# A hybrid decoder trunk on one core: three paddings that put the tensor engine's operands at one address modulo 512 bytes

## The chip, the cores and the metric

The kernel runs on one core of a Trainium2 chip. The metric is device time in microseconds (us) of one execution; the time before is 1634.1 us, the median of three runs between 1632.56 and 1635.3 us. TensorE (PE) multiplies, VectorE (DVE) and ScalarE (ACT) do the elementwise work, GpSimd (POOL) a little, and SyncE (SP) issues the loads and stores. The profile shows PE's weight loads as a row of their own (PEld).

## The reference

One decoder layer over 1024 rows of width 1024, then a final norm. All is float32.

```python
h = rms_norm(x, norm_mix)
proj = h @ w_in                      # 8 groups of 1024 columns: xa ga q f v g m_a m_b
xa = causal_depthwise_conv(xa, conv_w, conv_b)          # 4 taps
y_a = rg_lru(xa, w_r, b_r, w_i, b_i, lam) * gelu(ga)    # gates: 4 blocks of 256x256, then a scan
o = rms_norm(hgrn2_chunkwise(silu(q), k(f), log_f(f), v), hg_norm)
y = sigmoid(m_a) * y_a + sigmoid(m_b) * (o * silu(g))
x = x + y @ w_out
h = rms_norm(x, norm_mlp)
x = x + square(relu(h @ w_up)) @ w_down                 # width 4096 between
return rms_norm(x, norm_final)
```

## The kernel before, in words

**Three products for one.** Each float32 operand of the large products is split in two rounded parts: ScalarE writes the high part (L76), VectorE the rest (L77). `mm3` (L115, L116, L117) then issues three matmuls for one product: high with low, high with high, low with high. In `PE.matmul(o, a, b)` the operand `a` is the stationary one, which a weight load brings into the array (128 columns, 512 bytes of each partition), and `b` is the moving one, which is streamed through (512 columns, 2048 bytes of each partition, in nearly all of these matmuls; 256 columns for `pv`). A matmul's weight load runs while the matmul before it streams.

**The mixer** (tiles `pj_*`, `pv`, `pr`, `pi`, `sc`, `po`). Two chunks of 512 rows, in each four passes over 256 columns of every group. A projection (`pj_xa`, `pj_q`, `pj_f`, `pj_g`, `pj_mb`, `pj_ga`, `pj_ma`) has a slice of `w_in` (`wH`, `wL`) stationary and the transposed normed rows (`hT0H`, `hT0L`) moving. The convolution leaves its result in `xc`, split in `xcH` and `xcL`; these are the moving operand of the two gate products `pr` and `pi` of the recurrence (192 matmuls in all). The chunkwise mixer works with float32 matmuls that are not split (`sc`, `pk`, `pkv`, `po`). The output projection (`po`) has the mixer's result `y` stationary and the weights moving.

**The MLP** is done by Strassen's scheme in Winograd's form: seven products for eight, over 16 quads of the hidden width. In the first part (tiles `uX`, `uY`, `uZ`) the moving operands are the seven combinations of the normed rows (`h2B11`, `h2t1`, `h2T3` and so on, a high and a low tile each), which lie in four pools at the top of SBUF for the whole part; the stationary ones are the split weights (`wA..`, `ws..`) at its bottom. That is 16 quads x 7 steps x 4 x 3 = 1344 matmuls. In the second part (tiles `dX`, `dY`, `dZ`; 1344 matmuls again) two quads are accumulated together: three matmuls of the one quad, whose operands both lie in the lower pools, alternate with three of the other, whose operands both lie in pools at the top (`late_u`, `late_w`, `late_w1`). Here a `u` tile is stationary and a weight tile moving; VectorE adds each finished bank to the output rows `acc` (L963).

**Order and place.** The tile framework orders the instructions by the program's text and by priorities, and lays tiles in a pool one after the other; pools opened with `side="right"` are stacked downward from the top of SBUF. The tile `pad` (L674) is never read: it is opened first on that side and only shifts what is opened after it. The pool `mix` holds the mixer's tiles in the order of their first use: `mf` and `mu` come first, the two `xp` buffers of the convolution (L300) lie just before `xcH` and `xcL`.

Of the kernel before, what the change touches and what calls it, by code (L numbers as in the profile page):

```python
# [10 lines left out]
F32 = mybir.dt.float32  # L11
# [7 lines left out]
P = 128  # L19
D = 1024  # L20
S = 1024
T = 512
# [19 lines left out]
def trunk(ctx: ExitStack, tc: tile.TileContext, x, wts, mlp, pv, gains, mask_f, mask_u, out):  # L42
# [8 lines left out]
    def opened(name, **how):  # L51
        cm = tc.tile_pool(name=name, bufs=1, reuse_waits="tile", **how)
        return cm.__enter__(), lambda: cm.__exit__(None, None, None)
# [21 lines left out]
    def split(src, h, lo):  # L75
        keep(A.copy(h, src))  # L76
        keep(V.tensor_tensor(out=lo, in0=src, in1=h.bitcast(F32), op=ALU.subtract))  # L77
# [92 lines left out]
    def mt(tag, name, shape=(P, T), dt=F32, bufs=1):  # L170
        return m.tile(list(shape), dt, tag=tag, name=name, bufs=bufs)

    mf = mt("mf", "mf", (P, 32))
    mu = mt("mu", "mu", (P, 7, 8, 32), U8)

    def small_inputs():
# [93 lines left out]
    def project(c, name):  # L270

        pp = [bank("pj", f"pj_{name}_{s}") for s in range(2)]
        for half in range(2):
            wh, wl = next_w()
            for k in range(4):
                hh, hl = kt(hT[c], 4 * half + k)
                for s in range(2):
                    cols = slice(k * 256 + s * P, k * 256 + (s + 1) * P)
                    mm3(pp[s], wh[:, cols], wl[:, cols], hh, hl, half == 0 and k == 0, half == 1 and k == 3)
        return pp  # L280
# [15 lines left out]
    def conv(c, p, pp):  # L296
        xc = mt("xc", f"xc{c}{p}", (P, 2, T))
        for s in range(2):
            u = 2 * p + s
            xp = mt("xp", f"xp{c}{u}", (P, T + 3), bufs=2)  # L300
            V.tensor_copy(xp[:, 0:3], xcar[:, u, :])
            A.copy(xp[:, 3 : T + 3], pp[s])
            A.activation(
                xc[:, s, :],
                pp[s],
                AF.Identity,
                bias=pvt[:, PV_CB + u : PV_CB + u + 1],
                scale=pvt[:, PV_CW + 24 + u : PV_CW + 25 + u],
            )
            for j in range(3):  # L310
                V.scalar_tensor_tensor(  # L311
                    xc[:, s, :],
                    xp[:, j : j + T],
                    pvt[:, PV_CW + 8 * j + u : PV_CW + 8 * j + u + 1],
                    xc[:, s, :],
                    op0=ALU.mult,
                    op1=ALU.add,
                )
            if c + 1 < NC:
                G.tensor_copy(xcar[:, u, :], xp[:, T : T + 3])  # L320
        xh = mt("xcH", f"xcH{c}{p}", (P, 2, T), F32R)
        xl = mt("xcL", f"xcL{c}{p}", (P, 2, T), F32R)
        split(xc, xh, xl)
        return xc, xh, xl
# [43 lines left out]
    def f_of(c, p, pp):  # L368
        ff = mt("f", f"f{c}{p}", (P, 2 * T))
        kk = mt("kk", f"kk{c}{p}", (P, 2 * T))  # L370
        for s in range(2):
            u = 2 * p + s
            f, k = ff[:, s * T : (s + 1) * T], kk[:, s * T : (s + 1) * T]
            A.activation(f, pp[s], AF.Sigmoid)
            A.activation(k, pp[s], AF.Sigmoid, scale=-1.0)
            V.tensor_scalar(f, f, omlb[:, u : u + 1], lb[:, u : u + 1], op0=ALU.mult, op1=ALU.add)
            V.tensor_scalar(k, k, omlb[:, u : u + 1], None, op0=ALU.mult)
        V.tensor_scalar(ff, ff, F_MIN, 1.0, op0=ALU.max, op1=ALU.min)
        return ff, kk
# [246 lines left out]
    for c in range(NC):  # L626
        if c == 0:
            first_norm(0)
            mu32 = small_inputs()
        else:  # L630
            out_proj(0, ys, res0, done0, lambda: first_norm(1))
        ys = a2_set(a2y, f"y{c}")
        for p in range(NPAIR):
            v = project_v(c, f"{c}{p}")
            px = project(c, f"xa{c}{p}")
            if c == 0 and p == 0:
                parameters()
                tc.keep_in_program_order(V.tensor_copy(mu, mu32.to_broadcast([P, 7, 8, 32])))
            xc3 = conv(c, p, px)
            q1 = q_of(c, p, project(c, f"q{c}{p}"))  # L640
            f, kk = f_of(c, p, project(c, f"f{c}{p}"))
            with tc.high_priority(300):
                h = rg_lru(c, p, *xc3)
            on = hgrn(c, p, q1, f, kk, v)
            gates(c, p, h, on, ys)
# [25 lines left out]


    pad, close_pad = opened("pad", side="right")
    pad.tile([P, 8], F32, tag="pad", name="pad")  # L674

    h2p = [opened(f"h2{i}", side="right") for i in range(4)]
    HOME = {"T4": 0, "B22": 0, "T3": 0, "B21": 1, "n2": 2, "t1": 2, "B11": 3}
# [371 lines left out]
```

## Time and profile before

| | |
|---|---|
| median of 3 runs | 1634.1 us |
| span of the profiled execution, first to last instruction | 1630.3 us |
| time of a run beyond that span (median less span) | 3.8 us |
| PE busy | 1585.8 us, 9240 matmuls |
| PE weight loads busy | 1303.6 us, 9240 |
| VectorE busy | 1211.9 us |
| ScalarE busy | 762.2 us |
| GpSimd busy | 62.8 us |

The profiled execution's time is its span with some us around it, and these 3.8 us stand for them here. The span divides into the mixer with the two output projections (from 0 to about 985 us), the first part of the MLP (to about 1305) and the second (to the end). Matmuls are pipelined: the duration of one in a row (some 0.39 us) is longer than the time from its start to the next one's start (some 0.23 us), and it is the second that adds up to the span. Where two matmuls of the same shape follow their own kind without a wait, a longer start-to-start time shows as the same number of ns more in the duration.

### The profile page before, as it was taken

To read this page: it belongs to the slowest core of one execution; us is meant where nothing else is said; L and a number is where in the kernel's file an instruction comes from. 1 tells how busy PE (TensorE), PEld (TensorE's weight loads), DVE (VectorE), ACT (ScalarE), POOL (GpSimd) and SP (SyncE) were. 2 spreads that over 40 slices of the span, in tenths; PEclk is the share of its full clock that TensorE was granted. 3 is DMA by queue.
4 is the path that set the end of the run, shared out by engine and by line. 5 is a ranking of instruction groups with operands and counts; after the bars stand their busy time and mean duration, and the time that the engine had idled before them with its cause. 6 is when DMAs were issued, how large, how long until landed. Compare 5 with 4: busy or idle time off the path is not lost.

```text
span 1630.3 us, 23190 instructions
## 1 busy us (share of the span) xinstructions
PE 1585.8 (97%) x9240; PEld 1303.6 (80%) x9240; DVE 1211.9 (74%) x1751; ACT 762.2 (47%) x1186; POOL 62.8 (4%) x99
## 2 busy tenths in 40 slices
PE   7999999999999999999999998999999999999998
PEld 6788788788788788788787876888888878888886
DVE  5975956848764965848759688977777888888876
ACT  4643545435442544436435566767766732221113
POOL 0010100100100000000100000000000000000000
PEclk9999999999999999999999998999999999999999
DMA  6222223223244222222222352666666566666652
GB/s 236 91 66 91 91 66 103 66 91 93 78 165 142 80 77 91 78 84 98 66 91 91 125 200 102 262 247 239 233 248 247 216 259 237 238 246 249 252 207 104
DMA packets 57996, 246.51 MB, mean 151 GB/s; under 512 B 6688, under 2 KB 6816, under 8 KB 47136
## 3 DMA queue, kind: packets, MB, share of 16 engines
q1 hardware_dynamic: 56304, 239.27, 40.8%
q10 hardware_dynamic: 1584, 5.77, 1.0%
q8 instruction: 72, 1.18, 0.3%
q14 instruction: 36, 0.29, 0.1%
HBM read 185.24 MB, written 59.77 MB: 150 GB/s over the span
## 4 chain that ended last, share of the span: by engine, by line
PE 82%; DVE 15%; issue 1%; ACT 1%; DMA 1%; POOL 0%; DVEq 0%; POOLq 0%; SPq 0%; ACTq 0%
PE dX L115 4%; PE dX L117 4%; PE dX L116 4%; PE uX L115 3%; PE uX L117 3%; PE uX L116 3%; DVE wL L77 2%; PE pj_ga L117 2%; PE pj_ga L116 2%; PE pj_ga L115 2%; PE pj_ma L117 2%; PE pv L116 2%; PE pv L115 2%; PE pj_ma L116 2%; PE pv L117 2%; PE pj_f L117 2%
## 5 line engine op out<-in xcount | busy, mean ns | idle before, releaser
L77 DVE TENSOR_TENSOR wL<-raw,wH 128x1024 fp32r<-128x1024 f32 x160 | 194.4, 1215 | 151.3 <-ACT wH L76 148.7
L76 ACT CAST wH<-raw 128x1024 fp32r<-128x1024 f32 x160 | 167.9, 1050 | 166.9 <-issue 67.1
L963 DVE TENSOR_TENSOR acc<-acc,dX 128x512 f32<-128x512 f32 x128 | 86.7, 682 | 29.6 <-PE dX L117 28.9
L76 ACT CAST wA<-q 128x512 fp32r<-128x512 f32 x32 | 19.8, 621 | 130.9 <-PE dX L117 82.8
L963 DVE TENSOR_TENSOR acc<-acc,dY 128x512 f32<-128x512 f32 x64 | 43.6, 683 | 16.6 <-PE dY L117 14.9
L345 DVE RECIPROCAL rr<-rr 128x512 f32<-128x512 f32 x16 | 53.5, 3345 | 0.0
L823 ACT ACTIVATE b<-b 128x512 f32<-128x512 f32 x48 | 30.2, 631 | 38.7 <-DVE b L822 38.6
L115 PE MATMUL pv<-wL,hT0H 128*128 128x256 f32 x128 | 37.1, 289 | 0.0
L117 PE MATMUL pv<-wH,hT0L 128*128 128x256 f32 x128 | 36.7, 286 | 0.0
L116 PE MATMUL pv<-wH,hT0H 128*128 128x256 f32 x128 | 36.6, 286 | 0.0
L115 PE MATMUL pv<-wL,hT1H 128*128 128x256 f32 x128 | 36.5, 285 | 0.0
L116 PE MATMUL pv<-wH,hT1H 128*128 128x256 f32 x128 | 36.2, 283 | 0.0
L117 PE MATMUL pv<-wH,hT1L 128*128 128x256 f32 x128 | 36.2, 283 | 0.0
L311 DVE SCALAR_TENSOR_TENSOR xc<-xp,pvt,xc 128x512 f32<-128x512 f32 x48 | 33.1, 746 | 0.0
L551 ACT ACTIVATE on<-po 128x128 f32<-128x128 f32 x64 | 17.0, 278 | 33.5 <-PE po L541 33.2
L570 ACT ACTIVATE smb<-pj_mb 128x512 f32<-128x512 f32 x16 | 9.6, 597 | 45.4 <-PE pj_mb L117 45.2
L824 ACT ACTIVATE b<-b 128x512 f32<-128x512 f32 x48 | 30.0, 629 | 1.1
L384 DVE TENSOR_TENSOR seg<-seg 128x128 f32<-128x128 f32 (+2 forms) x96 | 26.8, 309 | 0.2
L565 ACT ACTIVATE g<-pj_g 128x512 f32<-128x512 f32 x16 | 9.6, 598 | 37.2 <-PE pj_g L117 37.2
L444 POOL TENSOR_SCALAR seg<-seg 128x128 f32<-128x128 f32 (+1 forms) x16 | 12.6, 790 | 360.9 <-DVE seg L384 360.9
L117 PE MATMUL pj_ga<-hT1H,wL 128*128 128x512 f32 x64 | 26.5, 414 | 0.0
L115 PE MATMUL uX<-h2B11L,wA 128*128 128x512 f32 x64 | 26.2, 409 | 0.3 <-DVE rstd_h L137 0.3
(1854 smaller groups left out, 5258.3 us busy)
## 6 DMA issues: line engine op xcount, KB each, us to landing
raw<-wts_in SPq DMA_DIRECT2D x160, 512.0 KB, 3.5
q<-mlp_in SPq DMA_DIRECT2D x64, 512.0 KB, 4.0
x<-x_in SPq DMA_DIRECT2D x8, 512.0 KB, 5.6
acc<-x ACTq DMA_DIRECT2D x8, 512.0 KB, 6.0
y_out<-acc SPq DMA_DIRECT2D x16, 256.0 KB, 2.1
xs<-x_in SPq DMA_DIRECT2D x8, 256.0 KB, 4.2
x<-xs SPq DMA_DIRECT2D x8, 256.0 KB, 2.1
x2s<-x_in SPq DMA_DIRECT2D x4, 512.0 KB, 4.8
```

Of the source, the lines that this page charges most:

```text
L76: keep(A.copy(h, src))
L77: keep(V.tensor_tensor(out=lo, in0=src, in1=h.bitcast(F32), op=ALU.subtract))
L115: PE.matmul(o, ah, bl, start=first, stop=False, **how)
L116: PE.matmul(o, ah, bh, start=False, stop=False, **how)
L117: PE.matmul(o, al, bh, start=False, stop=last, **how)
L311: V.scalar_tensor_tensor(xc[:, s, :], xp[:, j : j + T], pvt[:, PV_CW + 8 * j + u : PV_CW + 8 * j + u + 1], xc[:, s, :], op0=ALU.mult, op1= ...
L345: V.reciprocal(rec, rec)
L384: mul = lambda o, a, b: V.tensor_tensor(out=o, in0=a, in1=b, op=ALU.mult)
L551: A.activation(on[:, 4 * s + n, :], po[:, n * P : (n + 1) * P], AF.Square, accum_out=ssq[:, 4 * s + n : 4 * s + n + 1])
L823: A.activation(b[:, at, :], b[:, at, :], AF.Relu, scale=-1.0 if at == 2 else 1.0)
L824: A.activation(b[:, at, :], b[:, at, :], AF.Square)
L963: V.tensor_tensor(out=dst, in0=dst, in1=banks[bk, pr], op=op)
```

## The change

Three tiles grow. `mf` goes from 32 to 64 columns, of which the first 32 are used; each of the two `xp` buffers goes from T + 3 = 515 to T + 64 = 576 columns, of which the first 515 are used; `pad` goes from 8 to 56 columns, none of which is used.

```diff
-    mf = mt("mf", "mf", (P, 32))
+    mf = mt("mf", "mf", (P, 64))[:, 0:32]
...
-            xp = mt("xp", f"xp{c}{u}", (P, T + 3), bufs=2)
+            xp = mt("xp", f"xp{c}{u}", (P, T + 64), bufs=2)
...
     pad, close_pad = opened("pad", side="right")
-    pad.tile([P, 8], F32, tag="pad", name="pad")
+    pad.tile([P, 56], F32, tag="pad", name="pad")
```

Every engine issues the same instructions in the same order as before, with the same shapes and waits; only addresses differ. In the built programs the start addresses, modulo 512 bytes, are:

| tiles | before | after |
|---|---|---|
| `hT`, `y`, `wH`, `wL`, the lower pools' weights and `u` tiles, `raw`, `s`, `b`, `e` | 256 | 256 |
| `h2..` (moving operands of the MLP's first part) | 448 | 256 |
| the upper pools' weights and `u` tiles (one quad of two in the second part), `acc` | 448 | 256 |
| `xcH`, `xcL` (moving operands of `pr` and `pi`) | 192 | 256 |
| `q1`, `kk`, `qa`, `seg`, `dd`, `h`, `rw`, `ri`, `rr` | 192 | 256 |
| `x`, `xn`, `f`, `xc`, `v`, `kT`, `g1`, `g2`, `on`, `scT`, `tmp` | 128 | 256 |
| `sn` (moving in some `po`) | 256 | 320 |
| `ident` (moving in transposes) | 128 | 128 |

Counted from the bottom of a partition, `hT`, `y` and the operands of the lower pools lie below byte 113408, `xcH` and `xcL` from 170688, and `h2` and the operands of the upper pools from 114624 up.

All offsets of the split operands inside their tiles are multiples of 512 bytes, so each matmul of `mm3` starts its two operands where the table says: before, `pj` and `pv` at 256 and 256, `pr` and `pi` at 192 (moving) and 256, `u` at 448 (moving) and 256, `d` at 256 and 256 for the one quad and 448 and 448 for the other; after, all at 256 and 256.

## The prediction

> **What bounds the kernel now.** I read the page's totals first, then its chain of work that ended last.
>
> ```profile
> span 1630.3 us, 23190 instructions
> PE 1585.8 (97%) x9240; PEld 1303.6 (80%) x9240; DVE 1211.9 (74%) x1751; ACT 762.2 (47%) x1186; POOL 62.8 (4%) x99
> PEclk9999999999999999999999998999999999999999
> PE 82%; DVE 15%; issue 1%; ACT 1%; DMA 1%; POOL 0%; DVEq 0%; POOLq 0%; SPq 0%; ACTq 0%
> ```
>
> TensorE is the bound: 97% busy, at full clock, and 82% of the chain. The change removes no instruction and no wait, so it can only act through what a matmul takes. The next view is the groups of matmuls by line and shape: count, busy us, mean ns of one.
>
> ```profile
> L115 PE MATMUL pj_q<-hT0L,wH 128*128 128x512 f32 x64 | 24.9, 389 | 0.0
> L115 PE MATMUL pi<-xcL,wH 128*128 128x512 f32 x32 | 12.7, 395 | 0.0
> L115 PE MATMUL uY<-h2B22L,ws31H 128*128 128x512 f32 x4 | 1.6, 397 | 0.0
> L115 PE MATMUL dX<-wA,u3B 128*128 128x512 f32 x4 | 1.6, 401 | 0.0
> L116 PE MATMUL dX<-wA,u2B 128*128 128x512 f32 x4 | 1.6, 397 | 0.0
> L117 PE MATMUL dX<-wA,u2B 128*128 128x512 f32 x4 | 1.6, 396 | 0.0
> ```
>
> One shape, one kind of operand, and yet 389 ns in the projections against 395 to 401 in the gate products and in both parts of the MLP. These durations overlap; the cost is in the starts. The timeline of TensorE (start us, duration us) gives them: the first and the last of 48 `pj_ma` matmuls in a row, then the first and the last of 157 `u` matmuls in a row, then thirteen of the `d` part one after the other.
>
> ```profile
> 437.59 0.39 PE L115 MATMUL pj_ma<-hT0L,wH 128*128 128x512 f32 x1
> ...
> 448.24 0.39 PE L117 MATMUL pj_ma<-hT0H,wL 128*128 128x512 f32 x1
> ```
> ```profile
> 1204.65 0.39 PE L115 MATMUL uX<-h2T3L,ws310H 128*128 128x512 f32 x1
> ...
> 1241.05 0.39 PE L115 MATMUL uY<-h2B22L,ws312H 128*128 128x512 f32 x1
> ```
> ```profile
> 1402.03 0.39 PE L115 MATMUL dY<-ws318L,u2B 128*128 128x512 f32 x1
> 1402.26 0.40 PE L116 MATMUL dY<-ws318H,u2B 128*128 128x512 f32 x1
> 1402.49 0.40 PE L117 MATMUL dY<-ws318H,u2B 128*128 128x512 f32 x1
> 1402.73 0.40 PE L115 MATMUL dY<-ws319L,u3B 128*128 128x512 f32 x1
> 1402.97 0.39 PE L116 MATMUL dY<-ws319H,u3B 128*128 128x512 f32 x1
> 1403.19 0.39 PE L117 MATMUL dY<-ws319H,u3B 128*128 128x512 f32 x1
> ...
> 1404.82 0.39 PE L115 MATMUL dX<-wA1218L,u2t 128*128 128x512 f32 x1
> ```
>
> Start to start, a `pj_ma` matmul takes (448.24 - 437.59) / 47 = 226.6 ns, a `u` matmul (1241.05 - 1204.65) / 156 = 233.3 ns, and the twelve `d` matmuls (1404.82 - 1402.03) / 12 = 232.5 ns on the mean. The `u` matmuls thus pay 6.7 ns each. Set beside the table of addresses: all `pj` operands are at 256; the moving operand of `u` is at 448 and that of `pi` at 192, with weights at 256; and in `d` three matmuls at 256 take turns with three at 448, so that at each turn the weights of one residue are loaded while operands of the other stream. The cost in `d` isn't tied to one quad alone: the group of the lower quad's second matmul (`u2B`, L116) has 397 ns, that of the upper quad's first (`u3B`, L115) 401. I take the residue as the cause, and 226.6 ns as what a matmul comes down to when all residues are equal.
>
> The last question is where TensorE's pace sets the end. The windows give, for stretches of the MLP, length, busy us and count by engine.
>
> ```profile
> 985.00:1012.00 27.00, 24.23 (x98) 18.45 (x96) 22.91 (x33) 18.76 (x32) 0.71 (x2) 0.86 0.19 59
> 1012.00:1289.00 277.00, 276.96 (x1186) 222.35 (x1187) 221.04 (x273) 191.83 (x271) 0.00 (x0) 1.00 0.63 243
> 1289.00:1314.30 25.30, 23.90 (x102) 18.70 (x100) 25.09 (x33) 18.32 (x26) 0.00 (x0) 1.00 0.63 222
> 1314.30:1613.00 298.70, 298.66 (x1288) 241.84 (x1289) 238.44 (x347) 61.35 (x82) 0.00 (x0) 1.00 0.59 228
> ```
>
> In the second and fourth, TensorE is busy throughout and VectorE for 80% (221.04 of 277.00; 238.44 of 298.70): a TensorE 3% faster leaves VectorE at 82%. In the third VectorE is the bound (25.09 of 25.30), and in the first TensorE waits.
>
> **The change, part by part.**
>
> *`pad`, first part of the MLP.* `h2` moves from 448 to 256: 1186 matmuls in the window x 6.7 ns = 7.9 us, all on the path.
>
> *`pad`, second part.* The upper quad's operands move from 448 to 256. A window counts a matmul that only reaches into it, so the starts cover 298.70 + 0.39 us; 299.1 / 1288 = 232.2 ns, 5.6 over the base, and 1288 x 5.6 = 7.2 us on the path. The floor of this term is nothing (a rival below).
>
> *The 200 matmuls of the first and third windows* stand beside VectorE's chain: counted at 0, at most 200 x 6.7 ns = 1.3 us.
>
> *`mf` and `xp`: the gate products.* 192 matmuls x (395 - 389) = 1.2 us. The mixer's chain goes through VectorE too (its 15%), so I take half, 0.6 us; ends 0 and 1.2.
>
> *Other matmuls that shift.* After interruptions by small matmuls some projections are slow although both operands are at 256, such as `pj_mb`. I leave that as it is; the other end is that it goes with the small matmuls' residues, (398 - 389) x 384 = 3.5 us for `pj_mb`. The small ones themselves don't care: `poT` has both operands at 128, `pk` 128 and 192, `po<-v,scT` both at 128.
>
> ```profile
> L116 PE MATMUL pj_mb<-hT0H,wH 128*128 128x512 f32 x64 | 25.4, 398 | 0.0
> L538 PE MATMUL po<-v,scT 128*128 128x128 f32 x128 | 23.4, 275 | 0.0
> L525 PE MATMUL pk<-ident,kk 128*128 128x128 f32 x56 | 8.7, 273 | 0.0
> L586 PE MATMUL poT<-ident,on 128*128 128x128 f32 x64 | 8.3, 272 | 0.0
> ```
>
> *VectorE and ScalarE* read and write at the new addresses. The same split costs the same whether its three tiles are all at 256 (`wL`) or at 128 and 192 (`xcL`), so this is 0.
>
> ```profile
> L77 DVE TENSOR_TENSOR wL<-raw,wH 128x1024 fp32r<-128x1024 f32 x160 | 194.4, 1215 | 151.3 <-ACT wH L76 148.7 <-PE pj_ga L117 2.6
> L77 DVE TENSOR_TENSOR xcL<-xc,xcH 128x1024 fp32r<-128x1024 f32 x8 | 9.7, 1217 | 0.0
> ```
>
> *What is late next.* In seven of the quads a `uX` weight load waits for ScalarE's copy of the bank X (first row: us, times; then the load with its wait, and the copy).
>
> ```profile
>   PEld uX L115: 1.5, 7
> ```
> ```profile
> 1202.44 0.19 PEld L115 LDWEIGHTS uX<-h2T3L,ws310H 128*128 128x128 f32 x1 [0.23 <-ACT e L819]
> ```
> ```profile
> 1198.96 1.05 ACT L76 CAST ws111H<-s 128x1024 fp32r<-128x1024 f32 x1 [0.67 <-PE uX L116]
> ...
> 1201.82 0.58 ACT L819 COPY e<-uX 128x512 f32<-128x512 f32 x1
> ```
>
> ScalarE's work ahead of that copy starts on a TensorE event at 1198.96, some 15 matmuls earlier, and doesn't shorten: the wait can grow by 15 x 6.7 ns = 0.1 us, seven times 0.7; I take 0.5 us back. No wait elsewhere in the second and fourth window is TensorE's.
>
> Sum: 7.9 + 7.2 + 0.6 - 0.5 = 15.2 us. The span goes from 1630.3 to 1615.1, and with the 3.8 us around it the median from 1634.1 to 1618.9; I say 1619. With all upper ends (7.9 + 7.2 + 1.3 + 1.2 + 3.5 = 21.1) it is 1613.0.
>
> **The rivals.**
>
> *The place counts, not the residue: no change, 1634.* Every fast group has its operands in the lower half of SBUF (`hT`, `y`, lower weights), and every slow one has one in the upper half, or takes turns with one: `xc`, `h2`, the upper quad. The trace before can't tell this from the residue. Against it stand the 397 ns of `u2B` L116, a matmul with all operands low between two others of that kind. The Trainium skill, in "SBUF — State Buffer", section "Who interferes with whom", gives the same time by another way: TensorE has two independent read ports, one for the moving operand and one for the weight load, and never waits on anyone. By that rule addresses can't matter and the time is 1634; but it leaves the 389 and 397 ns of the same shape without a cause, so I don't weigh it higher than the place.
>
> *Only the first part gains: 1626.* If the `d` matmuls' 5.6 ns come from taking turns between four tiles and not from their residues, 7.9 + 0.6 - 0.5 = 8.0 us is all. For it: in `d` each matmul has its own two operands at one residue, and still the slowest intervals of all are there. Against it: in `d` the loads run ahead, so the residues that meet are those of neighbours, and two of six differ.
>
> *The equal residue is the bad case: slower.* ScalarE's and VectorE's splits in the MLP write and read at 256. If the 6.7 ns came from their meeting the weights, which lie at 256 too, then `h2` and the upper quad brought to 256 would meet them as well: as much again, (1186 + 1288) x 6.7 ns = 16.6 us, 1651. It decides from 3.3 / 2474 = 1.3 ns more per matmul. Against it: in the projections all matmul operands are at 256, the 160 splits of `wL` run beside them at 256, and `pj_q` stays at 389.
>
> **How the numbers follow.** Main case 0.66, only the first part 0.15, no change 0.14, slower 0.05. A difference within 0.2% (3.3 us) is about what a measurement of this kernel can't tell from none. Faster therefore 0.81, same 0.14, slower 0.05. The range leaves out the last two cases, 0.19: from 1613, all upper ends, to 1628, the first part alone with three quarters of its 7.9 us (5.9 + 0.6 - 0.5 = 6.0).
>
> **What would show it.** Right: `uY` groups and `dX` groups at 389 ns like `pj_q`, `pi` at 389, the two long windows shorter by about 8 and 7 us with the same counts, and the waits of `uX` for `e` somewhat longer. Wrong: `uY` still at 397 (place, not residue), `dX` still at 396 to 401 beside `uY` at 389 (turns, not residue), or `pj_q` above 389 (equal residues collide). It would also be wrong in size if VectorE's waits for TensorE turned round in these windows.

## The result, and the profile after

The changed kernel takes 1619.03 us (median of 4 runs, 1617.25 to 1621.08) against 1634.63 us before (4 runs; the 1634.1 given above was the median of three). The ratio is 0.9912, with a 95% interval of 0.9900 to 0.9924: 0.9% faster, where 1619 had been forecast in a range of 1613 to 1628. The span of the profiled execution is 14.8 us shorter.

The totals and the chain of waits on the page of the changed kernel:

```profile
span 1615.5 us, 23190 instructions
PE 1571.4 (97%) x9240; PEld 1303.4 (81%) x9240; DVE 1210.2 (75%) x1751; ACT 761.5 (47%) x1186; POOL 63.8 (4%) x99
PE 81%; DVE 15%; DMA 1%; issue 1%; ACT 1%; POOL 0%; DVEq 0%; POOLq 0%; SPq 0%
```

TensorE's busy time fell by 14.4 us with the same 9240 matmuls; weight loads, VectorE and ScalarE stayed within 2 us. Groups of matmuls of the changed kernel (count, busy us, mean ns), then two rows of the view of tile `u3B` (duration in ns, minimum/median/maximum):

```profile
L116 PE MATMUL pj_mb<-hT0H,wH 128*128 128x512 f32 x64 | 25.5, 399 | 0.0
L115 PE MATMUL pj_q<-hT0L,wH 128*128 128x512 f32 x64 | 24.9, 389 | 0.0
L115 PE MATMUL pi<-xcL,wH 128*128 128x512 f32 x32 | 12.5, 390 | 0.0
L115 PE MATMUL uY<-h2B22L,ws31H 128*128 128x512 f32 x4 | 1.6, 389 | 0.0
```
```profile
L115 PE MATMUL dX<-wA,u3B x4: 389/389/389, 1379.1 to 1399.5; 128*128 128x512 f32 x4
L116 PE MATMUL dX<-wA,u3B x4: 389/389/389, 1379.3 to 1399.7; 128*128 128x512 f32 x4
```

`uY` came from 397 to 389 ns, `dX` from 401 to 389, `pi` from 395 to 390, and `pj_q` stayed: these groups now cost what the projections cost. `pj_mb`, slow with equal residues, is as slow as it was; the small `sc` matmuls that interrupt it start at many offsets inside their tiles, and whether that is what slows it is open.

Where the time came off is read from three marks on TensorE's timeline: the first `u` matmul, the first and the last `dX`. Before:

```profile
988.88 0.79 PE L115 MATMUL uX<-h2B11L,wA 128*128 128x512 f32 x1 [0.31 <-DVE rstd_h L137]
1305.55 0.40 PE L115 MATMUL dX<-wA,u14B 128*128 128x512 f32 x1
1622.29 0.39 PE L117 MATMUL dX<-wA1229H,u13t 128*128 128x512 f32 x1
```

and after:

```profile
987.11 0.80 PE L115 MATMUL uX<-h2B11L,wA 128*128 128x512 f32 x1 [0.31 <-DVE h2B11L L77]
1296.69 0.39 PE L115 MATMUL dX<-wA,u14B 128*128 128x512 f32 x1
1607.72 0.39 PE L117 MATMUL dX<-wA1229H,u13t 128*128 128x512 f32 x1
```

The mixer gave 988.88 - 987.11 = 1.8 us, the first part of the MLP 316.67 - 309.58 = 7.1, the second 316.74 - 311.03 = 5.7.

### The profile page after: what moved, and what is told of

Its sections match the earlier page's. It is cut to its first block, busy times and chain, and to the rows that moved or that the text cites. A ratio compares the mean times of both kernels' runs of the same rounds, so it can differ in the third digit from the quotient of the medians.

```text
span 1615.5 us, 23190 instructions
## 1 busy us (share of the span) xinstructions
PE 1571.4 (97%) x9240; PEld 1303.4 (81%) x9240; DVE 1210.2 (75%) x1751; ACT 761.5 (47%) x1186; POOL 63.8 (4%) x99
## 4 chain that ended last, share of the span: by engine, by line
PE 81%; DVE 15%; DMA 1%; issue 1%; ACT 1%; POOL 0%; DVEq 0%; POOLq 0%; SPq 0%
PE dX L115 3%; PE dX L116 3%; PE dX L117 3%; PE uX L115 3%; PE uX L117 3%; PE uX L116 3%; DVE wL L77 2%; PE pj_ga L117 2%; PE pj_ga L116 2%; PE pj_ga L115 2%; PE pj_ma L116 2%; PE pj_ma L117 2%; PE pv L115 2%; PE pv L117 2%; PE pv L116 2%; PE pj_ma L115 2%
## 5 line engine op out<-in xcount | busy, mean ns | idle before, releaser
L384 DVE TENSOR_TENSOR kk<-kk,seg 128x768 f32<-128x768 f32 (+1 forms) x32 | 26.2, 819 | 0.3 <-DVE dd L438 0.3
```

Of the source, the lines that this page charges most:

```text
L384: mul = lambda o, a, b: V.tensor_tensor(out=o, in0=a, in1=b, op=ALU.mult)
```

## The experiments

The theory: what costs is the difference, modulo some power of two, between the address that one matmul streams from and the address that weights are loaded from beside it. Its rivals: absolute alignment to 256 bytes, each matmul's own two operands, a mere property of the order in the second part, and a meeting of TensorE's reads with those of VectorE and ScalarE. Times are compared with runs of the kernel before on the same chip.

### The pad alone

```diff
-    pad.tile([P, 8], F32, tag="pad", name="pad")
+    pad.tile([P, 56], F32, tag="pad", name="pad")
```

> Only pad grows; mf and xp stay, so xcH and xcL stay at 192 and the MLP's operands go to 256. Residue theory: u and d groups at 389 ns as in the changed kernel, pi stays at 395; the start of the first part of the MLP doesn't move (first u matmul near 989 us), and the two parts together give some 13 us, so about 1621 us, ratio near 0.992. If the parts of the change were not independent, u or d would keep some of their 6 ns.

Measured: 1622.1 us against 1632.79, ratio 0.9928 (0.9914 to 0.9941). Two groups of this kernel, a row of its view of tile `u3B`, and its first `u` matmul:

```profile
L115 PE MATMUL pi<-xcL,wH 128*128 128x512 f32 x32 | 12.7, 396 | 0.0
L115 PE MATMUL uY<-h2B22L,ws32H 128*128 128x512 f32 x4 | 1.6, 389 | 0.0
```
```profile
L115 PE MATMUL dX<-wA,u3B x4: 389/389/389, 1382.9 to 1403.3; 128*128 128x512 f32 x4
```
```profile
988.97 0.79 PE L115 MATMUL uX<-h2B11L,wA 128*128 128x512 f32 x1 [0.31 <-DVE rstd_h L137]
```

Both parts of the MLP come down to 389 ns, `pi` does not, and the mixer ends where it did before. The gain is 10.7 us on the medians, 10 to 14 by the interval, for an expected 13.

### The convolution's tiles alone

```diff
-    mf = mt("mf", "mf", (P, 32))
+    mf = mt("mf", "mf", (P, 64))[:, 0:32]
...
-            xp = mt("xp", f"xp{c}{u}", (P, T + 3), bufs=2)
+            xp = mt("xp", f"xp{c}{u}", (P, T + 64), bufs=2)
```

> Only mf and xp grow; pad stays. Residue theory: pi at 390 ns, u at 396 and d at 394 on the mean as before; the mixer ends some 1.2 us earlier (192 matmuls x 6 ns), total 1633 us, ratio near 0.999. If the mixer's 1.8 us of gain in the changed kernel came from VectorE or ScalarE at new addresses and not from these matmuls, it shows without a change of pi.

Measured: 1631.14 us against 1632.79, ratio 0.9991 (0.9982 to 0.9999).

```profile
L115 PE MATMUL pi<-xcL,wH 128*128 128x512 f32 x32 | 12.5, 389 | 0.0
L115 PE MATMUL dX<-wA,u3B 128*128 128x512 f32 x4 | 1.6, 401 | 0.0
L115 PE MATMUL uY<-h2B22L,ws314H 128*128 128x512 f32 x4 | 1.6, 397 | 0.0
```
```profile
987.39 0.80 PE L115 MATMUL uX<-h2B11L,wA 128*128 128x512 f32 x1 [0.31 <-DVE h2B11L L77]
```

`pi` comes down, `dX` and `uY` don't, and the MLP starts 1.5 us earlier than before. The two halves multiply to 0.9928 x 0.9991 = 0.9920, inside the interval of the whole change, as it would be with independent parts.

### All operands at 448

The kernel after, but with `pad` back at 8 columns and 192 bytes put at the bottom of SBUF, so that what lies at the bottom moves from 256 to 448 and no operand of `mm3` starts at 256 any more.

```diff
+    const.tile([P, 48], F32, tag="shift", name="shift")
     ident = const.tile([P, P], F32, tag="ident", name="ident")
...
-    pad.tile([P, 56], F32, tag="pad", name="pad")
+    pad.tile([P, 8], F32, tag="pad", name="pad")
```

> 192 bytes are put at the bottom of SBUF and pad stays at 8 columns: weights, hT, y, xc, h2 and both quads' operands all lie at 448 modulo 512. Relative theory (only the difference between the operand that streams and the weights being loaded counts): all groups at 389 ns as in the changed kernel, about 1619 us. Absolute theory (operands must start at a multiple of 256): u and d stay at 395 or more and the projections join them at 395, some 3400 more matmuls x 6.7 ns = 23 us, about 1657 us.

Measured: 1620.64 us against 1632.79, ratio 0.9921 (0.9907 to 0.9935).

```profile
L115 PE MATMUL pj_q<-hT0L,wH 128*128 128x512 f32 x64 | 24.9, 389 | 0.0
L115 PE MATMUL pi<-xcL,wH 128*128 128x512 f32 x32 | 12.4, 389 | 0.0
L115 PE MATMUL uY<-h2B22L,ws32H 128*128 128x512 f32 x4 | 1.6, 389 | 0.0
```

Here `h2` stands at the very bytes where it cost 397 ns before, and it costs 389, because the weights moved. The absolute theory falls, and with it what was left of the theory of the place in SBUF.

### Half as many turns in the second part

The layout of before; the loop over the two quads stands outside the loop over the two row blocks, so six matmuls of one quad run before six of the other.

```diff
-                for pr in prs:
...
-                    for i, q in enumerate(qs):
-                        wh, wl = ops_w[QUADS + q][wo]
-                        uh, ul = u_ops[q][uo]
...
+                for i, q in enumerate(qs):
+                    wh, wl = ops_w[QUADS + q][wo]
+                    uh, ul = u_ops[q][uo]
+                    for pr in prs:
...
```

> The layout of before, but in the second part of the MLP six matmuls of one quad run before six of the other, not three and three: half as many turns from one residue to the other. Neighbour theory (the load of the next matmul's weights meets the stream of the current one, and only a turn between residues costs): the excess per d matmul halves from 5.6 to about 2.8 ns, the second part is shorter by 3 to 4 us, about 1631 us. If what counts were each matmul's own addresses, the mean of d stays at 232 ns and the time at 1634.

Measured: 1630.42 us against 1632.79, ratio 0.9988 (0.9979 to 0.9997). The window from 1330 to 1590 us (length, then busy us and count, TensorE first), before and in this kernel:

```profile
1330.00:1590.00 260.00, 260.00 (x1123) 210.53 (x1122) 207.44 (x293) 49.26 (x54) 0.00 (x0) 1.00 0.62 239
```
```profile
1330.00:1590.00 260.00, 260.00 (x1129) 211.70 (x1128) 207.78 (x294) 51.46 (x54) 0.00 (x0) 1.00 0.62 241
```

With 260.4 us of starts, that is 231.9 and 230.6 ns per matmul, an excess of 5.3 and 4.0 over 226.6. The direction is right: no matmul's own addresses changed, only its neighbours, and the excess fell. So the theory of the own operands falls. VectorE's and ScalarE's addresses didn't change either, and in the trace before the `u` matmuls from 1020 to 1280 us take 233 ns both where VectorE is idle beside them and where it works throughout: nothing speaks for a meeting with other engines. The size isn't right: the excess did not halve, and the second part, from the first to the last `dX`, is 1.7 us shorter where 3 to 4 were expected. A turn costs 3 x 5.3 = 16 ns when three matmuls follow it and 6 x 4.0 = 24 ns when six do; read so, a disturbance goes on for more than three matmuls. The trace before shows something alike after an interruption by small matmuls, among `pj_ga` matmuls with both operands at 256:

```profile
432.12 0.39 PE L115 MATMUL pj_ga<-hT0L,wH 128*128 128x512 f32 x1
...
433.28 0.39 PE L117 MATMUL pj_ga<-hT0H,wL 128*128 128x512 f32 x1
...
433.96 0.39 PE L117 MATMUL pj_ga<-hT0H,wL 128*128 128x512 f32 x1
```

Five steps take 1.16 us, 232 ns each, and the three after them 0.68, 227 each. Whether it is the same thing isn't shown.

### The same order with equal residues

The loop of the last experiment in the changed kernel.

> The changed kernel with the second part in runs of six matmuls a quad instead of three. Neighbour theory: with equal residues a turn costs nothing, so d stays at 389 ns and the time at 1619 us. If the order of the matmuls and not the residues made the difference in the layout of before, this one is faster than the changed kernel by 1 to 2 us.

Measured: 1618.92 us, ratio 0.9913 (0.9895 to 0.9930), the changed kernel's ratio over again. That interval is too wide to rule out 1 to 2 us; the window of the second part decides:

```profile
1330.00:1590.00 260.00, 260.00 (x1148) 215.28 (x1147) 206.58 (x295) 56.24 (x67) 0.00 (x0) 1.00 0.59 231
```

260.4 / 1148 = 226.8 ns is the base. With equal residues a turn costs nothing, and the order by itself gains nothing.

### A sweep of the difference

Seven more values of `pad`, all else as before. They move `h2` (and the upper quad) to other distances from the weights at 256.

```diff
-    pad.tile([P, 8], F32, tag="pad", name="pad")
+    pad.tile([P, 48], F32, tag="pad", name="pad")    # 48 40 32 24 16 128 120
```

> Layout of before but pad of 48 columns: h2 and the upper quad at 288, a difference of 32 bytes to the weights at 256. If only equality counts: u at 233 ns start to start as at 192. If the cost has a width (the two reads collide over some number of bytes), a small difference may cost more or less than 192; a cost in steps of 64 bytes would leave 32 free, u at 226.6.

> pad of 40 columns: a difference of 64 bytes. If only equality counts: u at 233 ns and about 1634 us, as before. The gate products, at a difference of 448 (-64), had 233 ns, so a symmetric cost gives 233 here.

> pad of 32 columns: a difference of 96 bytes, the rest as before. So far the u matmuls' excess over 226.6 ns is 0 at differences of 0 and 256, 6.6 at 32, 2.3 at 64, 5.8 at 128 and 6.6 at 192. If the cost repeats every 256 bytes and each 32-byte step has its own: something between 2 and 7 ns here; if only multiples of 64 other than 0 are cheaper (bank lines of 64 bytes), 6.6 as at 32.

> pad of 24 columns: a difference of 128 bytes. If only equality modulo 512 counts: u at 233 ns, about 1634 us. If the modulus is 128: u at 226.6, about 1620 us.

> pad of 16 columns: a difference of 160 bytes. Period of 256: between 2 and 7 ns of excess per u matmul, 1629 to 1634 us.

> pad of 128 columns: h2 at 480, a difference of 224 bytes, which is -32 modulo 256. If the cost is symmetric, 6.6 ns of excess per u matmul as at 32, about 1633 us; if it isn't, less.

> pad of 120 columns: h2 and the upper quad at 0, a difference of 256 bytes. If the modulus is 256: u at 226.6 ns and about 1620 us; if it is 512: u at 233 ns or more, about 1634 us.

The window from 1020 to 1280 us, which lies in the first part of the MLP, of the kernel before (192), after (0), and of the runs at 32, 64, 96, 128, 160, 224 and 256, in this order:

```profile
1020.00:1280.00 260.00, 260.00 (x1115) 208.79 (x1114) 210.09 (x260) 181.01 (x254) 0.00 (x0) 1.00 0.64 245
```
```profile
1020.00:1280.00 260.00, 260.00 (x1143) 213.73 (x1142) 212.76 (x263) 184.06 (x262) 0.00 (x0) 1.00 0.65 253
```
```profile
1020.00:1280.00 260.00, 260.00 (x1115) 208.16 (x1114) 210.10 (x259) 180.91 (x255) 0.00 (x0) 1.00 0.63 245
```
```profile
1020.00:1280.00 260.00, 260.00 (x1133) 212.01 (x1132) 212.36 (x262) 182.64 (x257) 0.00 (x0) 1.00 0.65 250
```
```profile
1020.00:1280.00 260.00, 260.00 (x1115) 208.38 (x1113) 209.97 (x259) 180.95 (x254) 0.00 (x0) 1.00 0.63 245
```
```profile
1020.00:1280.00 260.00, 260.00 (x1118) 209.65 (x1117) 210.67 (x260) 181.50 (x255) 0.00 (x0) 1.00 0.63 245
```
```profile
1020.00:1280.00 260.00, 260.00 (x1111) 208.76 (x1110) 209.19 (x258) 180.07 (x254) 0.00 (x0) 1.00 0.63 245
```
```profile
1020.00:1280.00 260.00, 260.00 (x1115) 208.65 (x1114) 209.93 (x260) 181.09 (x254) 0.00 (x0) 1.00 0.63 245
```
```profile
1020.00:1280.00 260.00, 260.00 (x1143) 213.67 (x1142) 214.16 (x264) 183.72 (x261) 0.00 (x0) 1.00 0.65 251
```

260.4 us over the first count is the mean time per `u` matmul. At 0, 64 and 256 some 0.6 ns of it come from six or seven steps of over 0.30 us, waits for `e` (next section); before there is none in this window.

| moving less stationary address | ns per `u` matmul | ratio to before, 95% interval |
|---|---|---|
| 0 (the changed kernel) | 227.8 | 0.9912 (0.9900 to 0.9924) |
| 32 | 233.5 | 1.0000 (0.9989 to 1.0011) |
| 64 | 229.8 | 0.9981 (0.9970 to 0.9993) |
| 96 | 233.5 | 1.0004 (0.9994 to 1.0015) |
| 128 | 232.9 | 0.9987 (0.9975 to 0.9998) |
| 160 | 234.4 | 1.0003 (0.9992 to 1.0014) |
| 192 (before) | 233.5 | 1 |
| 224 | 233.5 | 0.9996 (0.9985 to 1.0007) |
| 256 | 227.8 | 0.9930 (0.9908 to 0.9953) |

At 256 the cost is gone as at 0, and the ratio is that of the pad alone: the period in this sweep is 256 bytes, not 512, and 128 isn't one. In between the cost is 5 to 7 ns, but for +64, with 2. This isn't symmetric: `u` at 192, which is -64 modulo 256, has the full 6 ns. Differences of less than 32 bytes weren't tried.

In the second part +64 gains nothing. The window from 1330 to 1590 us at 64:

```profile
1330.00:1590.00 260.00, 260.00 (x1122) 210.16 (x1121) 206.01 (x291) 50.12 (x56) 0.00 (x0) 1.00 0.61 235
```

Before it holds 1123 matmuls, at 256 it holds 1147, and at the other differences 1117 to 1127. There the turns go both ways, so that +64 and -64 both occur. What the run at 64 gains, it gains in the first part.

## Why the prediction was right

**The cause.** The residue as the cause, and 226.6 ns as the base, held: the slow groups that were named came down to 389 or 390 ns. That the trace before couldn't tell residue from place was true; moving `h2` by 192 bytes, or the weights instead, told it. The rule of two independent read ports from which TensorE never waits ("SBUF — State Buffer", section "Who interferes with whom" in the Trainium skill) would have given 1634; the sweep and the kernel with all operands at 448 show a matmul's pace going with the difference between where it streams from and where the weights beside it lie, so for these two streams the measurement decides against it. What inside the chip makes the two meet is not shown.

**First part of the MLP: 7.9 less 0.5 taken, 7.1 measured.** The rate gained all of 6.7 ns: the 156 steps that the prediction measured at 36.40 us take 35.36. What is late next was the wait that had been named: weight loads of `uX` for ScalarE's copy `e`, before 1.5 us in seven, in the changed kernel 2.1 in the same seven and 2.6 with one more.

```profile
  PEld uX L115: 2.6, 8
```

**Second part: 7.2 taken, 5.7 measured.** This term was too large by its rate and by its waits, about half each. The rate: the window behind the 232.2 ns begins with a wait, for TensorE starts nothing in it until 1314.34. From 1330 to 1590 us the starts are 231.9 ns apart before (1123 matmuls), and in the changed kernel

```profile
1330.00:1590.00 260.00, 259.61 (x1146) 214.53 (x1145) 207.72 (x298) 56.71 (x73) 0.00 (x0) 1.00 0.58 226
```

260.4 / 1146 = 227.2, or 226.7 without the wait shown next. So the rate gained 5.1 to 5.2 ns, some 6.6 us on 1288 matmuls. The waits: "No wait elsewhere in the second and fourth window is TensorE's" is the sentence that failed. A `u` tile had not landed:

```profile
1344.91 0.39 PE L117 MATMUL dY<-ws117H,u1t 128*128 128x512 f32 x1
1345.69 0.47 PE L115 MATMUL dX<-ws116L,u0n 128*128 128x512 f32 x1 [0.39 <-DMA u0n<-u0n]
```
```profile
1345.66 0.19 PEld L115 LDWEIGHTS dX<-ws116L,u0n 128*128 128x128 f32 x1 [0.78 <-DVE acc L963]
```

That is 0.78 us from start to start for 0.23, so 0.55 us given back; the remaining 0.3 us lies in smaller waits. The weight load's wait, put down to VectorE's `acc`, is the same gap and not a second one. Most of it comes from the transfer and not from the faster TensorE: `u0n` was issued 5.8 us ahead of its use before and 5.7 here, and landed after 4.9 us before, after 6.3 here. In the run at 256 bytes, of the same order and pace, it landed after 4.9 us, and this step is only 0.16 us late, with the weight load waiting for `acc`. At the slow pace, in the run at 160 bytes, it took 6.5 us and the wait is there:

```profile
L115 PE MATMUL dX<-ws116L,u0n 128*128 128x512 f32 x4 | 1.7, 413 | 0.4 <-DMA u0n<-u0n 0.4
```

**The mixer: 0.6 taken, 1.8 measured.** Half of 192 x 6 ns was too careful; all of the 1.2 us was on the path: at the last `pi` matmul the changed kernel and the one with the convolution's tiles alone are both 1.2 us ahead of the kernel before. The other 0.6 is one wait for VectorE's norm ahead of the MLP, before and after:

```profile
944.88 1.06 PE L704 MATMUL xT_h<-ident,xn_h 128*128 128x128 f32 x8 [1.34 <-DVE xn_h L139]
```
```profile
943.10 1.06 PE L704 MATMUL xT_h<-ident,xn_h 128*128 128x128 f32 x8 [0.73 <-DVE xn_h L139]
```

It differs from run to run whatever the pads: the step from the matmul before it takes 1.73 us in the kernel before, 1.12 in the changed one and 0.73 in the run at 96 bytes. I don't put it to the change.

The MLP gave 1.8 us less than the 14.6 taken for it and the mixer 1.2 more: the misses nearly cancel, and that 1619 was hit more closely than its terms was luck. `pj_mb` kept its 399 ns: its end of 3.5 us did not come, and its residues were equal from the start.

**The rivals.** No change fell with the result. Only the first part: the pad alone brought both parts to 389. Equal residues with the splits as the bad case: `pj_q`, `pi`, `uY` and `dX` stand at 389 to 390 with the operands of `mm3` at 256, and at 389 with them at 448.

## What to carry to other kernels

When matmuls of one shape show two durations, put the start addresses of what streams and of the weights being loaded side by side: here differences of 0 and 256 bytes were free and every other multiple of 32 between them cost 2 to 3% of a 512-column matmul, but for +64. It is one kernel and one kind of matmul. The cost lies between neighbours in TensorE's order, so all operands of a stage belong at one residue, not only each pair; a few hundred bytes of padding ahead of a pool did it here. Before counting the gain, take the rate from a stretch without waits, and look for evacuations that only just end in time, as ScalarE's copy `e` did, because a faster TensorE turns some of its gain into waits.

## What the runs showed that I had not expected

The period of 256 bytes, where the change aims at 512: a pad that left the upper tiles at 0 did as well as the one that took them to 256. The cheap +64 beside the dear -64 and 32. And the memory of a disturbance: one turn between residues slows several matmuls after it, 16 to 24 ns in all, so that halving the turns took away only a quarter of the excess (5.3 to 4.0 ns). And one load, `u0n`, took from 4.8 to 7.7 us to land over the fourteen traces, and made TensorE wait at either pace.
